# Six weight tiles of lead instead of five for the first token tile in the second block

## The chip, the cores and the metric

The kernel runs on one core of one Trainium2 chip. The metric is the device time of one execution in microseconds (us), from the first to the last instruction of the core with what lies around them. The engines are named as the profile names them: PE (TensorE, matmuls), PEld (its weight loads), DVE (VectorE), ACT (ScalarE), POOL (GpSimd) and SP (SyncE, which issues most of the transfers).

## What is computed

Two transformer blocks stand behind one another, each of two layers, over 256 tokens of width 1024. The change touches only the second. It is, with every matmul in full float32 precision:

```python
def second_block(x, norm_gains, w_ffn_gate, w_ffn_up, w_ffn_down, w_in, w_out, diff_lambda, diff_subln_gain):
    for layer in range(DEPTH):                       # DEPTH = 2
        g = norm_gains[layer]
        h = rmsnorm(x, g[0])
        x = x + 0.5 * rmsnorm(swiglu(h, w_ffn_gate[layer, 0], w_ffn_up[layer, 0], w_ffn_down[layer, 0]), g[1])
        h = rmsnorm(x, g[2])
        x = x + rmsnorm(token_mixer(h, w_in[layer], w_out[layer], ...), g[3])
        h = rmsnorm(x, g[4])
        x = x + 0.5 * rmsnorm(swiglu(h, w_ffn_gate[layer, 1], w_ffn_up[layer, 1], w_ffn_down[layer, 1]), g[5])
    return x
```

swiglu is (silu(h Wg) * (h Wu)) Wd with an inner width of 2816. token_mixer projects h to queries, keys and values, runs three kinds of attention over them (dilated, differential, stick-breaking: attn_a, attn_b and attn_c in the code), and multiplies what they give by w_out.

## The kernel before, in words

**Token tiles and weight tiles.** The 256 tokens are two token tiles of 128, t0 and t1. All weights of both blocks lie in one stream of weight tiles of 128 x 1024 numbers, in the order of use. Tiles 0 to 63 belong to the first block. In the second block tiles 64 to 129 are the first FFN of layer 0, 130 to 161 its mixer (24 tiles of w_in, then 8 of w_out), 162 to 227 its second FFN, and 228 to 391 the same for layer 1. Each weight tile is used by t0 and by t1. Float32 precision comes from splitting: a weight tile arrives by DMA as `raw`, ACT casts it to its high part `whi`, and DVE subtracts to get the low part `wlo` (Stream.convert, line 341). One use of a weight tile by one token tile is then six matmuls of 512 columns: twice high by high, low by high and high by low. Below this is called a pass. In the names `u0`, `m0` and `y0` a matmul writes for t0 (`u` gate and up, `m` mixer projection, `y` down or output projection), and `u1`, `m1` and `y1` for t1.

**Slots.** Eight converted weight tiles fit in memory in the second block (WBUFS = 4 and WMORE = 4). Tile n takes the slot of tile n - 8, so its cast waits until t1, which comes last, has used tile n - 8. Four raw tiles can be under way (RAWB = 4).

**Who sets the order.** Sched (line 167) is a planner that runs when the kernel is built. It holds one generator for each token tile and a list of side jobs (norms, swiglu, attention), and an estimated clock for each engine. Each round it lets one token tile issue its next pass. Among those that may, the one in the earlier stage (`phase`) goes first, and within a stage t0. A token tile may not start a pass when it would be `lead` or more weight tiles ahead of the last one:

```python
                if pos[t] < len(W.widths):
                    if pos[t] - lo >= self.lead or pos[t] >= W.nconv:
                        continue
```

`pos[t]` is the next weight tile of t, `lo` the smaller of the two, and `W.nconv` the number of tiles converted so far. LEAD is 5. What the planner writes is the program's order; the framework below it then makes one queue for each engine, in which an instruction that it takes to be ready can come ahead of one that it takes to wait. Each engine works through its queue in that order.

**The seams.** At the end of an FFN or of the mixer each token tile goes through `norms` (line 497) and `prenorm` (line 454): ACT sums the squares of the two halves of y (`junk`), DVE multiplies y by the gains (`u_post`), computes a reciprocal root in some nine dependent instructions of one column (`rw`, `rs_y`, `rs_h`, `rs_t`), and adds to the residual (`x`); PE transposes x (`tpx`), DVE scales (`h_f`), ACT casts (`h_hi`), DVE subtracts (`h_lo`), and only then can PE start the next stage for this token tile. Conversions during this time are held to three tiles ahead of t0 (QUIET = 3). In the mixer, attn_b (line 865) ends with the matmuls `avb`, a chain on DVE over `o_b`, the transpose `tpm` and the parts `m_hi` and `m_lo`, on which the weight tiles 160 and 161 (layer 0) or 324 and 325 (layer 1) wait. In the FFN, swiglu (line 558) makes `sg`, transposes it (`tpg`) and splits it into `g`.

Of the kernel before, what the change touches and what calls it, by code (L numbers as in the profile page):

```python
# [1852 lines left out]
LEAD, WBUFS, WMORE, RAWB, W2, QZ, S4 = (5,4,4,4,10,2,16)  # L1853
# [3 lines left out]
def build(tc, a, wst, widths, n1, tab, ident, cols, rows, lamp, out):  # L1857
    nc = tc.nc
    with ExitStack() as ctx:
        def pool(name, bufs, **k):  # L1860
            return ctx.enter_context(tc.tile_pool(name=name, bufs=bufs, **k))


        pool("pad", 1).tile([P, PADS[0] // 4], F32, name="pad")
        wp, hp, work, rawp, cp = pool("wp", WBUFS), pool("hp", 2), pool("work", 2), pool("rawp", RAWB), pool("const", 1)
        small, psA = pool("small", 2), pool("psA", 1, space=PSUM)

        class PS:
            def tile(self, shape, dt, tag, name):
                return psA.tile(shape, dt, tag=tag, name=name, bufs={"ps": 6, "tp": 2}[tag])  # L1870

        X = [cp.tile([P, D], F32, name=f"x{t}") for t in range(2)]
        ones = cp.tile([P, P], F32, name="ones")
        nc.gpsimd.memset(ones, 1.0)
        idn = cp.tile([P, P], F32, name="ident")
        nc.gpsimd.dma_start(idn, ident)
        cl = cp.tile([P, cols.shape[1]], F32, name="cols")
        nc.gpsimd.dma_start(cl, cols)
        lp = cp.tile([P, 128], F32, name="subln")
        st = Stream(tc, wst, widths, rawp, wp, WBUFS, RAWB)  # L1880
        S = Sched(tc, st, LEAD)
        ps = PS()
        one = ExitStack()
        p1 = one.enter_context(tc.tile_pool(name="first", bufs=1, reuse_waits="tile"))
        first = First(tc, S, X, cl, idn, ones, ps, work, small, hp, p1, a, [0, n1 // 2])
        second = Second(tc, S, X, cl, rows, idn, lp, ones, out, ps, work, small, hp)
        first.end = second.first
        left = [0, 1]

        def main(t):  # L1890
            yield from first.main(t)
            left.remove(t)
            if not left:
                assert all(x[1].__name__ == "prenorm" for x in S.sides), S.sides
                one.close()
                p2 = ctx.enter_context(tc.tile_pool(name="second", bufs=1, reuse_waits="tile"))
                second.open(p2, tab)
                second.lambdas(lamp[:, :256])
                st.widen(st.alloc(p2, WMORE), WMORE)
                st.rawb = RAWB  # L1900
            yield from second.main(t)

        first.consts()
        S.spawn(first.start())
        st.widen(lambda i: [first.s4([P, 1024], f"w{n}{i}", F32R) for n in range(2)], WX[0], WX[1], WX[2])
        mains = {t: main(t) if t < 2 else first.main(t) for t in range(4)}
        nc.gpsimd.dma_start(lp, lamp[:, 256:].to_broadcast([P, 128]))
        S.run(mains)
# [37 lines left out]
```

## Time and profile before

| | us |
|---|---|
| median of 3 runs | 1449.67 (1449.08 to 1450.29) |
| the profiled execution | 1447.77 |
| its span, first to last instruction | 1446.0 |
| PE busy | 1403.1 (97%) |
| DVE busy | 1002.7 (69%) |
| ACT busy | 765.8 (53%) |
| start of the second block in the span | about 426 |

The busy time of PE counts a matmul from its start to its modelled end. Matmuls overlap: one of 512 columns shows about 0.39 us but the next starts 0.23 us later, so time on PE is best read from the starts of neighbouring matmuls. Most of the arithmetic goes through two helper lines (L230 matmuls, L221 DVE, L216 ACT), so the rows below are told apart by the names of the tiles.

### The profile page before, as it was taken

The page shows a single profiled execution, that of the slowest core. Times are in us where ns is not written, and L with a number is a line of the kernel's source. Part 1 is how long each engine was busy: PE and PEld are TensorE (multiplying, and loading weights), DVE is VectorE, ACT ScalarE, POOL GpSimd, SP SyncE. Part 2 cuts the span into 40 slices and gives each one's busy share as a digit, 9 for nine tenths or more (in the row PEclk, how much of TensorE's full clock was granted, in tenths as well). Part 3 has the DMA queues.
Part 4 walks back from the last instruction along what each step waited for, and adds up shares of the span by engine and source line. Part 5 has one row for each costly group of instructions (what it writes and reads, how often), then busy time and mean ns, then how long its engine had stood idle before and what let it go on. Part 6 is the DMA issues. An engine that isn't in the chain of part 4 may idle for free.

```text
span 1446.0 us, 19092 instructions
## 1 busy us (share of the span) xinstructions
PE 1403.1 (97%) x6766; PEld 1134.5 (78%) x6766; DVE 1002.7 (69%) x2175; ACT 765.8 (53%) x1348; POOL 30.0 (2%) x46
## 2 busy tenths in 40 slices
PE   7999997999999999999999999999999999999997
PEld 4778886777877888777878888788887778788886
DVE  4899978779787555587886555765555878865554
ACT  4465533576565444567655444554445676554442
POOL 1000000000000000000000000000000000000000
PEclk9999999999999999999999999999999999999999
DMA  8751455333456555653446566566566534466551
GB/s 304 238 172 59 128 192 162 123 124 121 159 189 209 186 188 188 190 186 121 139 139 204 189 180 186 173 193 187 188 189 189 182 125 134 143 200 186 185 186 58
DMA packets 69088, 245.64 MB, mean 170 GB/s; under 512 B 7841, under 2 KB 8097, under 8 KB 68865
## 3 DMA queue, kind: packets, MB, share of 16 engines
q1 hardware_dynamic: 66384, 235.11, 51.1%
q0 software_dynamic: 2176, 8.79, 1.8%
q8 instruction: 53, 0.87, 0.2%
q10 hardware_dynamic: 432, 0.53, 0.1%
q14 instruction: 43, 0.34, 0.1%
HBM read 243.35 MB, written 1.05 MB: 169 GB/s over the span
## 4 chain that ended last, share of the span: by engine, by line
PE 79%; DVE 11%; DMA 4%; ACT 3%; issue 2%; SPq 0%; DVEq 0%; ACTq 0%
PE u L230 37%; PE y L230 18%; PE m L230 9%; DMA raw<-in_wst_dram 3%; PE yo L230 3%; DVE adaj L221 2%; DVE wlo L221 2%; PE av L230 2%; PE tpg L234 2%; DVE acc L221 1%; ACT whi L216 1%; PE tpp L234 1%; DMA ada<-in_adan_dram 1%; PE sc L230 1%; ACT f L216 1%
## 5 line engine op out<-in xcount | busy, mean ns | idle before, releaser
L221 DVE TENSOR_TENSOR wlo<-raw,whi 128x1024 fp32r<-128x1024 f32 (+1 forms) x380 | 459.2, 1211 | 341.8 <-ACT whi L216 339.4
L216 ACT CAST whi<-raw 128x1024 fp32r<-128x1024 f32 (+1 forms) x380 | 395.3, 1042 | 386.7 <-PE u L230 228.5
L230 PE MATMUL u<-whi,h_hi 128*128 128x512 f32 x704 | 281.2, 400 | 1.1 <-ACT h_hi L216 1.1
L230 PE MATMUL u<-whi,h_lo 128*128 128x512 f32 x704 | 275.0, 391 | 0.6 <-DVE h_lo L221 0.6
L230 PE MATMUL u<-wlo,h_hi 128*128 128x512 f32 x704 | 275.5, 392 | 0.0
L230 PE MATMUL y<-whi,g 128*128 128x512 f32 x704 | 218.3, 390 | 0.5 <-ACT g L216 0.5
L230 PEld LDWEIGHTS y<-whi,g 128*128 128x128 f32 x704 | 132.0, 188 | 28.8 <-ACT g L216 0.8
L230 PEld LDWEIGHTS u<-wlo,h_hi 128*128 128x128 f32 x704 | 132.1, 188 | 27.7
L230 PEld LDWEIGHTS u<-whi,h_lo 128*128 128x128 f32 x704 | 132.5, 188 | 27.1 <-DVE h_lo L221 2.5
L230 PEld LDWEIGHTS u<-whi,h_hi 128*128 128x128 f32 x704 | 132.2, 188 | 26.4 <-ACT h_hi L216 1.7
L230 PE MATMUL y<-wlo,g 128*128 128x512 f32 x352 | 137.3, 390 | 0.0
L230 PE MATMUL u<-whi,hhi 128*128 128x512 f32 (+2 forms) x256 | 98.7, 388 | 0.4 <-ACT whi L216 0.3
L221 DVE CUSTOM_DVE_ANT_0 adaj<-ada,cbc 128x1024 bf16<-128x1024 f32 x76 | 90.6, 1221 | 8.7 <-DMA ada<-in_ada_dram 8.6
L230 PE MATMUL u<-wlo,hhi 128*128 128x512 f32 (+2 forms) x256 | 94.4, 372 | 0.4 <-DVE wlo L221 0.4
L230 PE MATMUL u<-whi,hlo 128*128 128x512 f32 (+2 forms) x256 | 94.8, 372 | 0.0
L230 PE MATMUL m<-whi,h_hi 128*128 128x512 f32 x192 | 79.0, 415 | 0.4 <-ACT h_hi L216 0.4
L230 PEld LDWEIGHTS y<-wlo,g 128*128 128x128 f32 x352 | 66.1, 188 | 14.3
L230 PE MATMUL m<-wlo,h_hi 128*128 128x512 f32 x192 | 75.5, 395 | 0.0
L230 PE MATMUL m<-whi,h_lo 128*128 128x512 f32 x192 | 75.3, 394 | 0.0
L221 DVE SCALAR_TENSOR_TENSOR acc<-glu,cw,acc 128x512 f32<-128x512 f32 (+1 forms) x120 | 70.8, 613 | 0.0
L230 PEld LDWEIGHTS u<-whi,hhi 128*128 128x128 f32 x256 | 48.2, 189 | 8.3 <-issue 1.9
L230 PEld LDWEIGHTS u<-wlo,hhi 128*128 128x128 f32 x256 | 48.2, 188 | 8.0 <-DVE wlo L221 1.2
(294 smaller groups left out, 1961.6 us busy)
## 6 DMA issues: line engine op xcount, KB each, us to landing
raw<-in_wst_dram SPq DMA_DIRECT2D x376, 512.0 KB, 3.6
ada<-in_ada_dram SPq DMA_DIRECT2D x42, 512.0 KB, 4.3
grow<-in_rows_dram POOLq DMA_DIRECT2D x10, 512.0 KB, 5.1
raw<-in_wst_dram SPq DMA_DIRECT2D x8, 416.0 KB, 3.1
ada<-in_adan_dram SPq DMA_DIRECT2D x6, 512.0 KB, 5.3
raw<-in_wst_dram SPq DMA_DIRECT2D x8, 256.0 KB, 2.8
tab<-in_tab_dram POOLq DMA_DIRECT2D x1, 1536.0 KB, 8.4
x<-in_x_dram SPq DMA_DIRECT2D x2, 512.0 KB, 5.4
```

Of the source, the lines that this page charges most:

```text
L216: ins = getattr(self.nc.scalar, fn)(*a, **k)
L221: ins = getattr(self.nc.vector, fn)(*a, **k)
L230: self.nc.tensor.matmul(*a, **k)
L234: self.nc.tensor.transpose(out, in_, ident)
```

## The change

The planner's lead becomes 6 when the second block opens. Nothing else is edited.

```diff
                 st.widen(st.alloc(p2, WMORE), WMORE)
                 st.rawb = RAWB
+                S.lead = LEAD + 1
             yield from second.main(t)
```

The instructions of the second block are the same as before in number; their order is not. In the long middle of an FFN the two token tiles still alternate pass by pass, with t0 six tiles ahead instead of five. The order moves most at the seams.

**At the end of the first FFN of layer 0, on PE:** t0 ends with weight tile 129. Before:

```order
L230 MATMUL y0_0_4740<-whi129_5840,g_5853 128x512 x2
L230 MATMUL y0_0_4740<-wlo129_5841,g_5853 128x512
L230 MATMUL y0_1_4741<-whi129_5840,g_5853 128x512 x2
L230 MATMUL y0_1_4741<-wlo129_5841,g_5853 128x512
L230 MATMUL u1_5856<-whi125_5755,h_hi_4462 128x512
```

After:

```order
L230 MATMUL y0_0_4740<-whi129_5852,g_5841 128x512 x2
L230 MATMUL y0_0_4740<-wlo129_5853,g_5841 128x512
L230 MATMUL y0_1_4741<-whi129_5852,g_5841 128x512 x2
L230 MATMUL y0_1_4741<-wlo129_5853,g_5841 128x512
L230 MATMUL u1_5862<-whi124_5743,h_hi_4462 128x512
```

Behind t0's last pass t1 goes on with tile 124 instead of 125. Up to the transposes `tpx` of t0 four passes of t1 stand in the queue (124 to 127) instead of three. The last two of t1 (128 and 129) stand behind m0's tiles 130 to 133 instead of behind tile 130 and half of 131; and between t1's last pass and its own `tpx` there are now 5 matmuls, the four transposes `tpqk`, two passes and 2 matmuls (19 matmuls in all), where there were 25 matmuls.

**At the same seam, on DVE:** from the residual `x0` of t0 to the first conversion behind its norm. Before:

```order
L221 SCALAR_TENSOR_TENSOR x0_80<-u_post_5918,rs_y_5924,x0_80 128x512
L221 SCALAR_TENSOR_TENSOR x0_80<-u_post_5920,rs_y_5924,x0_80 128x512
L221 SCALAR_TENSOR_TENSOR h_f_5965<-tpx_5960,cols_86 128x512
L221 SCALAR_TENSOR_TENSOR h_f_5974<-tpx_5969,cols_86 128x512
L221 TENSOR_TENSOR h_lo_5938<-h_f_5965,h_hi_5937 128x512
L221 TENSOR_TENSOR h_lo_5938<-h_f_5974,h_hi_5937 128x512
L221 TENSOR_TENSOR wlo133_5992<-raw133_5863,whi133_5991 128x1024
```

After:

```order
L221 SCALAR_TENSOR_TENSOR x0_80<-u_post_5906,rs_y_5912,x0_80 128x512
L221 SCALAR_TENSOR_TENSOR x0_80<-u_post_5908,rs_y_5912,x0_80 128x512
L221 TENSOR_TENSOR wlo132_5936<-raw132_5850,whi132_5935 128x1024
L221 SCALAR_TENSOR_TENSOR sg_5945<-u1_5862,first_4637,sg_5945 128x256
L221 SCALAR_TENSOR_TENSOR h_f_5965<-tpx_5960,cols_86 128x512
L221 SCALAR_TENSOR_TENSOR h_f_5974<-tpx_5969,cols_86 128x512
L221 TENSOR_TENSOR h_lo_5926<-h_f_5965,h_hi_5925 128x512
L221 TENSOR_TENSOR h_lo_5926<-h_f_5974,h_hi_5925 128x512
L221 TENSOR_TENSOR wlo133_5986<-raw133_5869,whi133_5985 128x1024
```

The conversion of tile 132 and the `sg` of t1, which stood ahead of `x0`, now stand between `x0` and `h_f`. Further on, the two root chains (t0's second norm and t1's first), which stood interleaved with one another and with both `u_post` of t1, now follow one after the other, with the conversion of tile 136 and both `u_post` between them. The seam between the layers (tile 227) and the end of layer 1's first FFN (tile 293) are changed in the same way.

**At the end of the mixer of layer 0, on PE:** the transposes of t1's residual. Before, with t1's last matmul (`y1_1<-wlo161`) 38 matmuls ahead of the first row of `tpx`:

```order
L230 MATMUL u0_7370<-whi168_7296,h_hi_7222 128x512
L230 MATMUL u0_7370<-whi168_7296,h_lo_7223 128x512
L234 MATMUL tpx_7383<-ident_84,x1_81 128x128 x4
L230 MATMUL u0_7370<-wlo168_7297,h_hi_7222 128x512
L234 MATMUL tpx_7392<-ident_84,x1_81 128x128 x4
```

After:

```order
L230 MATMUL y1_1_7094<-wlo161_7034,m_hi_6998 128x512
L234 MATMUL tpg_7347<-ident_84,sg_7326 128x128
L230 MATMUL u0_7379<-whi168_7337,h_hi_7170 128x512
L230 MATMUL u0_7379<-whi168_7337,h_lo_7171 128x512
L230 MATMUL u0_7379<-wlo168_7338,h_hi_7170 128x512
L230 MATMUL u0_7379<-whi168_7337,h_hi_7170 128x512
L230 MATMUL u0_7379<-whi168_7337,h_lo_7171 128x512
L230 MATMUL u0_7379<-wlo168_7338,h_hi_7170 128x512
L230 MATMUL u0_7379<-whi169_7388,h_hi_7170 128x512
L230 MATMUL u0_7379<-whi169_7388,h_lo_7171 128x512
L234 MATMUL tpx_7398<-ident_84,x1_81 128x128 x4
L234 MATMUL tpx_7407<-ident_84,x1_81 128x128 x4
```

Behind t1's last pass there are now 8 matmuls of t0 ahead of t1's transposes instead of 38: t0's passes over tiles 162 to 167 stand ahead of t1's passes 160 and 161 now, where they stood behind them. Tiles 168 and 169 take the slots of 160 and 161.

**At the same seam, on DVE:** where the tail of t1's attn_b stands. Before:

```order
L221 TENSOR_TENSOR wlo163_7138<-raw163_6977,whi163_7137 128x1024
L221 TENSOR_TENSOR o_b_7156<-avb_7147,rdB_6869 128x2x64 x2
L221 TENSOR_TENSOR sq_b_7159<-o_b_7156 128x256
L221 TENSOR_REDUCE ssB_7161<-sq_b_7159 128x4
L221 TENSOR_SCALAR ssB_7161<-ssB_7161 128x4
```

After:

```order
L221 TENSOR_TENSOR h_lo_7171<-h_f_7219,h_hi_7170 128x512
L221 TENSOR_TENSOR wlo165_7231<-raw165_7101,whi165_7230 128x1024
L221 TENSOR_TENSOR wlo166_7237<-raw166_7134,whi166_7236 128x1024
L221 TENSOR_TENSOR wlo167_7243<-raw167_7181,whi167_7242 128x1024
L221 TENSOR_TENSOR o_b_7259<-avb_7250,rdB_6919 128x2x64 x2
L221 SCALAR_TENSOR_TENSOR rw_7296<-ss_7223 128x1
```

The tail of t1's attn_b, which stood ahead of t0's norm, now stands behind it and behind the conversions of tiles 165 to 167. The end of layer 1's mixer is changed in the same way.

## Rows read from the trace of the kernel before

**Rows 1.** The page: busy time of PE, share of the span.

```profile
PE 1403.1 (97%) x6766; PEld 1134.5 (78%) x6766; DVE 1002.7 (69%) x2175; ACT 765.8 (53%) x1348; POOL 30.0 (2%) x46
```

**Rows 2.** Windows: stretch, its length, busy us by engine (instructions), PE clock, DMA share.

```profile
core 0: us, PE busy (x) PEld busy (x) DVE busy (x) ACT busy (x) POOL busy (x), PEclk, DMA share, GB/s
425.00:608.00 183.00, 181.53 (x817) 147.15 (x816) 107.00 (x166) 88.78 (x119) 2.37 (x3) 1.00 0.62 199
608.00:631.00 23.00, 21.88 (x104) 17.28 (x103) 22.36 (x59) 13.74 (x29) 1.58 (x3) 1.00 0.65 222
...
616.00:631.00 15.00, 15.00 (x73) 12.52 (x73) 14.77 (x41) 7.14 (x17) 0.83 (x2) 1.00 0.70 245
...
631.00:734.70 103.70, 103.02 (x550) 83.41 (x550) 79.96 (x235) 68.12 (x131) 5.73 (x6) 1.00 0.42 132
734.70:755.70 21.00, 20.10 (x97) 16.28 (x96) 20.56 (x57) 12.05 (x25) 0.53 (x1) 1.00 0.49 160
755.70:924.00 168.30, 168.30 (x758) 137.06 (x757) 91.27 (x114) 81.73 (x109) 0.00 (x0) 1.00 0.60 188
```

**Rows 3.** Timeline, end of the first FFN, PE: start us, us, instruction [idle before].

```profile
607.97 0.39 PE L230 MATMUL u<-whi,h_hi 128*128 128x512 f32 x1
...
609.33 0.62 PE L230 MATMUL y<-whi,g 128*128 128x512 f32 x2
...
612.95 1.29 PE L234 MATMUL tpx<-ident,x 128*128 128x128 f32 x8 [0.74 <-DVE x L221]
...
615.01 0.73 PE L230 MATMUL m<-whi,h_hi 128*128 128x512 f32 x2 [0.21 <-ACT h_hi L216]
615.74 0.50 PE L230 MATMUL m<-whi,h_lo 128*128 128x512 f32 x1
```

**Rows 4.** The same stretch, DVE.

```profile
607.66 1.23 DVE L221 TENSOR_TENSOR wlo<-raw,whi 128x1024 fp32r<-128x1024 f32 x1 [1.49 <-ACT whi L216]
608.81 1.28 DVE L221 SCALAR_TENSOR_TENSOR u_post<-y,grow 128x512 f32<-128x512 f32 x2
...
610.77 0.48 DVE L221 SCALAR_TENSOR_TENSOR sg<-u,first,sg 128x256 f32<-128x256 f32 x1
...
612.05 1.41 DVE L221 SCALAR_TENSOR_TENSOR x<-u_post,rs_y,x 128x512 f32<-128x512 f32 x2
613.62 1.35 DVE L221 SCALAR_TENSOR_TENSOR h_f<-tpx,cols 128x512 f32<-128x512 f32 x2
```

**Rows 5.** The same stretch, ACT: squares of t0's first half, end of the second.

```profile
606.58 1.05 ACT L216 CAST whi<-raw 128x1024 fp32r<-128x1024 f32 x1 [1.67 <-PE u L230]
607.53 0.59 ACT L216 ACTIVATE junk<-y 128x512 bf16<-128x512 f32 x1
...
608.66 0.20 ACT L216 ACTIVATION_READ_ACCUMULATOR junk<-y 128x1 f32 x1
```

**Rows 6.** Timeline, end of the first mixer, PE.

```profile
734.71 0.39 PE L230 MATMUL y<-whi,m_hi 128*128 128x512 f32 x1
...
740.18 0.63 PE L234 MATMUL tpx<-ident,x 128*128 128x128 f32 x4 [0.90 <-DVE x L221]
...
755.71 0.40 PE L230 MATMUL u<-whi,h_hi 128*128 128x512 f32 x1
```

**Rows 7.** Timeline, the same seam, DVE: t1's attention tail, t0's norm, conversions.

```profile
732.17 0.49 DVE L221 TENSOR_TENSOR o_b<-avb,rdB 128x128 f32<-128x128 f32 x2 [1.43 <-PE avb L230]
...
738.32 0.42 DVE L221 TENSOR_TENSOR o_b<-o_b,subln 128x256 f32<-128x256 f32 x1
...
743.77 4.63 DVE L221 TENSOR_TENSOR wlo<-raw,whi 128x1024 fp32r<-128x1024 f32 x4
```

**Rows 8.** Timeline, the first block, PE: a long wait.

```profile
221.87 1.09 PE L234 MATMUL tpy<-ident,y 128*128 128x128 f32 x4 [3.54 <-DVE y L221]
```

**Rows 9.** Windows behind that wait of PE, and around a shorter one.

```profile
220.00:225.00 5.00, 3.13 (x10) 2.63 (x11) 5.00 (x10) 1.31 (x4) 0.00 (x0) 0.66 0.79 224
...
400.00:405.00 5.00, 3.17 (x21) 2.16 (x19) 3.14 (x9) 4.86 (x13) 0.00 (x0) 1.00 0.90 302
```

## The prediction

> **What bounds the kernel now.** I read the page first: PE is busy for 97% of the span [rows 1], so only its waits can be won or lost. The windows say where they are. In the long middle of an FFN PE never rests: 168.30 us of 168.30 [rows 2], and the stretches from 947 to 1114 us and from 1262 to 1434 us read the same. The change cannot win anything there. What is open lies at five seams: three ends of an FFN (608 to 631 us; those from 924 and from 1114 us read alike, PE lacking 1.1 us in each) and two ends of a mixer (734.7 to 755.7 us; 1241.2 to 1262.2 us is its twin, 0.9 us each) [rows 2]. The reader is to see the DVE column there: 22.36 of 23 us and 20.56 of 21 us. At a seam DVE is as full as PE, since two norms and the conversions meet on it; elsewhere it is at half load. PE gets through a seam nearly without loss because enough passes stand in its queue while DVE works. Last come the timelines of one seam of each kind [rows 3 to 7], which carry the sum.
>
> **Prices.** A pass is 609.33 - 607.97 = 1.36 us [rows 3]. A conversion takes 1.05 us on ACT, then 1.23 us on DVE [rows 4, 5], 2.3 us together. The norm of a token tile takes from the first u_post to x 3.24 us (612.05 - 608.81; about 2.95 without the sg inside) and to tpx 4.1 us [rows 3, 4]. From h_f to the first matmul that reads h_lo it is 615.74 - 613.62 = 2.1 us [rows 3, 4].
>
> **The middle of the FFN: 0.** With a lead of 6, a weight tile's slot is freed four passes (5.4 us) before t0 needs the new tile, where it was six (8.2 us). The 2.3 us conversion is the work under this cover. Were the cover gone, each of the 328 tiles would cost what is missing; 3 us of it remain, so I take nothing. swiglu stands as far behind its unit as before.
>
> **An FFN's end.** Time 0 is the end of t0's last pass (607.97 in the trace).
> - *t0's norm.* Before, PE comes to the matmul with h_lo at 7.77 us. Of this, three passes (4.1), ten transposes (1.1) and two matmuls (0.45) are work, so about 2.1 us are lost. After, the cover is four passes (5.4 us), one conversion less stands before u_post, which can start at about 1.0, and x is done at 5.4. So tpx no longer waits: 0.9 us gained. But a conversion (1.2 us) and sg (0.5 us) now stand on DVE between x and h_f, where nothing stood: h_f starts at 7.1 to 7.4, the matmul with h_lo at 9.3, with 7.0 us of work. Lost: 2.3 to 2.5. The gain is given back: +0.3.
> - *t1's norm.* Before it costs nothing: PE is busy for 15.00 of the 15 us from 616 us [rows 2], since 25 matmuls stood ahead of tpx. After, 19 matmuls and four transposes do: 4.8 us. What is needed is longer. u_post must wait for the conversion of tile 136, which waits for t1's pass over 128: it starts 1.1 us after t1's last pass. With 3.0 us to x, a copy of 0.6 us inside the chain, and 0.9 us to tpx, that is 5.6 to 5.9: 1.0 us lost. Then DVE has x's second half (0.5) and a conversion (1.2) before h_f, and 2.1 us more to h_lo: 3.9 us after tpx, under which there are 2.0 us of work (eight transposes, 5 matmuls). Another 1.9. Sum 3.0.
> So +3.3 for each of the two seams into a mixer. At the seam between the layers sg and g of the next FFN stand in DVE's queue as well: +3.8. **Together +10.4.** From below, t1's part can be nearly 0 (if DVE interleaves in time what the queue has in a row); from above it is all of t1's norm uncovered, about 4 us. I keep 5 to 15 for the three.
>
> **A mixer's end.** Time 0 is the end of t0's last pass (734.71). Before, t1 starts its FFN at 755.71 [rows 6]; of the 21.0 us thirteen passes (17.7) and 18 transposes (2.0) are work: 1.3 us lost, nearly all at tpx [rows 6]. After, by steps:
> 1. t0's norm: u_post starts at 1.5 (scores of attn_b and a conversion precede it), tpx at 5.6, four passes 5.4: 0.2.
> 2. tile 164's conversion stands before h_f: 3.9 us from tpx to the matmul with h_lo, 2.2 us of work: 1.7. The last two avb wait on ACT behind both squares: 0.3.
> 3. t1's attention tail on DVE now follows h_lo (4.5 us after tpx) and three conversions (3.5 us; 4.63 for four [rows 7]), so o_b starts at 8.0. It took 738.74 - 732.17 = 6.6 us before, with a conversion and both u_post inside (2.5): 4.1. tpm at 12.2; PE arrives at 12.1: 0.1. Then m_hi and m_lo: 1.0.
> 4. t0 meanwhile stops at tile 167, since 168 takes the slot of 160, which t1 has not used. After t1's pass over 160 the conversion takes 2.3 us against 1.9 us of work: 0.4.
> 5. t1's norm: on ACT the cast of 169 and g come before the squares (1.05, 0.4 and 1.3 us; squares and cast in [rows 5]), so u_post starts 1.9 and ends 3.1 us after t1's last pass, x comes 2.0 later, tpx at 6.0. Work until then: 2.4 us with the wait of step 4, where there were 38 matmuls (8.6 us). Lost: 3.6. Then, as at the FFN's end, a conversion before h_f: 1.9.
> Sum 9.2, less 1.3: +7.9, twice **+15.8**. From below: were tpm as early as before, steps 3 and 4 fall away and step 5 halves, +4 each. From above: 1.2 us more for the root chains that share DVE in step 3 and 1.3 for x's second half, +10.5 each. So 8 to 21.
>
> **Inside the mixers and at the start.** The order shifts there too, and no row of before shows a weight tile that came late. From below, PE's lack inside a mixer is 0.7 us [rows 2], so at most 1.4 for both can be won, and 1.5 between 425 and 608 us. From above, the two conversions that follow t1's start have 3.2 us of work as cover and a root chain of 2 us ahead of them on DVE: up to 2 us each. I take 0, nearest to the rows, and keep -3 to +4.
>
> **Sum.** 10.4 + 15.8 = 26.2 us. The profiled execution took 1447.77 us (span 1446.0 and 1.8 around it), so 1474; the median of the runs lies 1.9 us above it, so **1476**.
>
> **The rivals.**
> - *Faster, 1444 us.* The fourth pass of t1 covers t0's norm at all five seams, and nothing comes late in its place. Won: 1.2 us (0.9 and the break in tpx) at each of three seams, 1.1 at two, 5.8 in all. It decides at t1's tpx: if x of t1 is there within 4.8 us of its last pass at an FFN's end and 2.4 us at a mixer's end. For it speaks that waits for x are the largest of PE's waits; against it that no norm in these rows runs in under 4.1 us from u_post alone. 7%.
> - *Slower by less, 1466 us.* The mixers' ends cost what I say, the FFN ends even out because DVE finds gaps for the conversions. DVE at 97% before [rows 2] speaks against it. 22%.
> - *Slower by more, 1480 us.* The wait of 3.6 us in step 5 lowers PE's clock. In the first block PE waited 3.54 us, and the stretch of 5 us behind it has a mean clock of 0.66; the one from 245 us, behind a like wait, reads the same, while the stretch from 400 us, with 1.8 us idle in it, stays at 1.00 [rows 8, 9]. [...] 22%.
> [...]
> - *No change.* That the lead would not bind is excluded by the order, in which t0 stands six ahead; that all shifts cancel: 4%.
>
> **How the numbers follow.** The forecast itself 45%, the rivals as given. Faster by over 0.2% (about what a measurement of this kernel can tell from no change) 0.07, within 0.2% 0.04, slower 0.89. The range runs from the lower bounds with part of the gain inside (+8, 1458) to the upper bounds with the clock (+38, 1488); it leaves out the faster case and no change, 1 in 10, and some of the tails.
>
> **What would show it.** In the windows, the middles of the FFNs stay at full PE. Each of three FFN ends shows a wait of tpx for x near t1's norm, which was not there, and none at t0's first tpx but one for h_hi behind it. Each mixer's end shows waits for tpm's m_hi, for whi or wlo of 168, and one of over 3 us at t1's tpx. If t1's tpx waits under 1 us there, step 5 is wrong and the result lies near 1460; if conversions show up as PE's releasers in the middle of the FFNs, the cover of 3 us was an illusion and the result is above the range.

## The result and the profile after

The changed kernel takes 1467.54 us (median, 1464.85 to 1467.97) against 1449.38 in the same comparison: ratio 1.0122, interval 1.0105 to 1.014. It is 18 us slower.

The page's busy times, after; before is in [rows 1]:

```profile
span 1465.8 us, 19121 instructions
...
PE 1415.2 (97%) x6766; PEld 1138.2 (78%) x6766; DVE 1011.8 (69%) x2175; ACT 763.3 (52%) x1348; POOL 30.0 (2%) x46
```

Each engine runs as many instructions as before, and the shares hardly move. The page can't tell where 20 us of span went; the windows can. After, the stretches that answer to [rows 2], cut at the same places in the work (columns as there):

```profile
core 0: us, PE busy (x) PEld busy (x) DVE busy (x) ACT busy (x) POOL busy (x), PEclk, DMA share, GB/s
428.50:609.90 181.40, 179.48 (x803) 144.97 (x802) 104.77 (x163) 87.45 (x118) 2.38 (x3) 1.00 0.61 196
609.90:637.00 27.10, 24.74 (x113) 18.79 (x112) 25.11 (x59) 15.03 (x31) 1.59 (x3) 1.00 0.65 208
637.00:735.90 98.90, 98.82 (x525) 80.14 (x524) 77.58 (x222) 64.85 (x126) 5.73 (x6) 1.00 0.42 134
735.90:766.20 30.30, 26.49 (x124) 20.76 (x122) 25.56 (x72) 15.69 (x31) 0.53 (x1) 0.94 0.40 126
766.20:933.30 167.10, 167.10 (x750) 135.54 (x749) 89.77 (x111) 79.11 (x104) 0.00 (x0) 1.00 0.59 186
```

PE still never rests in the middle of an FFN (167.10 of 167.10 us from 766.2 us on). It lacks 2.36 us at the FFN's end, where it lacked 1.12, and 3.81 us at the mixer's end, where it lacked 0.90; the clock column there reads 0.94. Inside the mixer the lack fell from 0.68 to 0.08.

**A ledger by equal work.** A matmul is known, by its place in the kernel's order, by its weight tile and token tile, so its start can be compared between two traces, each counted from the first matmul of the second block. These first matmuls are, before and after:

```profile
426.05 0.48 PE L230 MATMUL u<-whi,h_hi 128*128 128x512 f32 x1
```

```profile
428.47 0.48 PE L230 MATMUL u<-whi,h_hi 128*128 128x512 f32 x1
```

The 2.4 us between them arose in the first block, which no edit here reorders; in the profiles of this study that start lies between 424.1 and 428.7 us. So a median says no more than some 2 us about the second block, and the ledger, from one profile of each kernel, says more. Where t1 is one weight tile further behind at the marker, a pass (1.36 us) is taken off; with lead 4, where it is one tile less behind, a pass is added. The table gives the us lost against before, from t1's matmuls with tiles 116, 140, 214, 280, 304 and 380; the sum goes on to the block's last matmul, so it holds what lies behind tile 380 as well:

| kernel | start | FFN end, layer 0 | mixer 0 | seam of layers | FFN end, layer 1 | mixer 1 | sum |
|---|---|---|---|---|---|---|---|
| forecast | 0 | 3.3 | 7.9 | 3.8 | 3.3 | 7.9 | 26.2 |
| changed kernel | 1.2 | 2.2 | 5.0 | 2.3 | 1.8 | 4.9 | 17.4 |

From the start of the second block to its last matmul it is 1029.4 us after and 1012.0 before: 17.4. So all five seams lose, as forecast, each less than forecast.

**The waits of PE in the second block, after:**

```profile
engine line waited for: us in total, times, longest us
PE tpx L234 <- DVE x L221: 7.6, 5, 3.2
PE tpg L234 <- DVE h_f L221: 2.8, 3, 0.9
...
PE u L230 <- DVE h_lo L221: 1.1, 4, 0.3
PE u L230 <- DVE wlo L221: 0.9, 3, 0.4
PE m L230 <- DVE wlo L221: 0.8, 2, 0.4
```

Two of the five waits for x are the long ones behind the mixers, three are t1's at the FFN ends. The transposes tpg that wait for h_f stand right behind t0's tpx.

**An FFN's end, DVE, after** (t0's last pass ends at 610.15, t1's at 627.0):

```profile
613.98 1.42 DVE L221 SCALAR_TENSOR_TENSOR x<-u_post,rs_y,x 128x512 f32<-128x512 f32 x2
615.32 1.22 DVE L221 TENSOR_TENSOR wlo<-raw,whi 128x1024 fp32r<-128x1024 f32 x1
616.45 0.48 DVE L221 SCALAR_TENSOR_TENSOR sg<-u,first,sg 128x256 f32<-128x256 f32 x1
616.85 1.28 DVE L221 SCALAR_TENSOR_TENSOR h_f<-tpx,cols 128x512 f32<-128x512 f32 x2
...
626.74 1.23 DVE L221 TENSOR_TENSOR wlo<-raw,whi 128x1024 fp32r<-128x1024 f32 x1 [0.91 <-ACT whi L216]
627.88 1.28 DVE L221 SCALAR_TENSOR_TENSOR u_post<-y,grow 128x512 f32<-128x512 f32 x2
...
631.45 1.41 DVE L221 SCALAR_TENSOR_TENSOR x<-u_post,rs_y,x 128x512 f32<-128x512 f32 x2
632.78 1.22 DVE L221 TENSOR_TENSOR wlo<-raw,whi 128x1024 fp32r<-128x1024 f32 x1
634.03 1.29 DVE L221 SCALAR_TENSOR_TENSOR h_f<-tpx,cols 128x512 f32<-128x512 f32 x2
```

and PE there:

```profile
615.60 1.03 PE L234 MATMUL tpx<-ident,x 128*128 128x128 f32 x8
617.58 0.44 PE L234 MATMUL tpg<-ident,sg 128*128 128x128 f32 x2 [0.95 <-DVE h_f L221]
...
618.96 0.50 PE L230 MATMUL m<-whi,h_lo 128*128 128x512 f32 x1
...
632.35 1.29 PE L234 MATMUL tpx<-ident,x 128*128 128x128 f32 x8 [0.36 <-DVE x L221]
634.05 0.50 PE L230 MATMUL m<-wlo,h_hi 128*128 128x512 f32 x1 [0.42 <-DVE wlo L221]
```

The reader is to see three conversions (`wlo`) in the norms' chains: between t0's x and h_f, ahead of t1's u_post, and behind t1's x.

**A mixer's end, PE, after:**

```profile
753.30 0.41 PE L234 MATMUL tpm<-ident,o_b 128*128 128x128 f32 x2 [0.19 <-DVE o_b L221]
...
754.17 0.74 PE L230 MATMUL y<-whi,m_hi 128*128 128x512 f32 x2 [0.23 <-ACT m_hi L216]
...
758.01 0.50 PE L230 MATMUL u<-wlo,h_hi 128*128 128x512 f32 x1 [0.23 <-DVE wlo L221]
...
762.83 1.94 PE L234 MATMUL tpx<-ident,x 128*128 128x128 f32 x8 [3.16 <-DVE x L221]
```

t1's passes 160 and 161 stand here behind tpm; [rows 6] had t0's tpx at this place with 0.90. Then t1's tpx waits 3.16 us, and the window behind it runs at half clock (0.50); from 765.9 to 771 us the granted clock is 1.00 again:

```profile
762.50:765.90 3.40, 3.08 (x11) 2.73 (x12) 3.25 (x6) 1.46 (x4) 0.00 (x0) 0.50 0.46 123
```

### The profile page after: what moved, and what is told of

It reads as the page before. It is cut to its first block, busy times and chain, and to the rows that moved or that the text cites. A ratio compares the mean times of both kernels' runs of the same rounds, so it can differ in the third digit from the quotient of the medians.

```text
span 1465.8 us, 19121 instructions
## 1 busy us (share of the span) xinstructions
PE 1415.2 (97%) x6766; PEld 1138.2 (78%) x6766; DVE 1011.8 (69%) x2175; ACT 763.3 (52%) x1348; POOL 30.0 (2%) x46
## 4 chain that ended last, share of the span: by engine, by line
PE 72%; DVE 15%; ACT 5%; DMA 5%; issue 2%; SPq 0%; DVEq 0%; ACTq 0%
PE u L230 33%; PE y L230 17%; PE m L230 8%; DVE wlo L221 3%; DMA raw<-in_wst_dram 3%; PE yo L230 3%; DVE adaj L221 2%; ACT whi L216 2%; PE tpg L234 2%; PE av L230 1%; DVE acc L221 1%; DVE rs_t L221 1%; DVE x L221 1%; DVE rs_y L221 1%; DMA ada<-in_adan_dram 1%
## 5 line engine op out<-in xcount | busy, mean ns | idle before, releaser
L230 PE MATMUL u<-whi,h_hi 128*128 128x512 f32 x704 | 275.8, 392 | 0.3 <-ACT h_hi L216 0.2
L230 PE MATMUL y<-whi,g 128*128 128x512 f32 x704 | 224.1, 399 | 0.5 <-ACT g L216 0.5
L230 PEld LDWEIGHTS y<-whi,g 128*128 128x128 f32 x704 | 126.9, 188 | 23.9 <-ACT g L216 0.7
```

Of the source, the lines that this page charges most:

```text
L230: self.nc.tensor.matmul(*a, **k)
```

## The experiments

Lead by place is written as a function `at` of the weight tile that a token tile is about to use:

```diff
-                    if pos[t] - lo >= self.lead or pos[t] >= W.nconv:
+                    if pos[t] - lo >= self.at(pos[t]) or pos[t] >= W.nconv:
```

The ledger of all eleven runs, in us against before as above (for three of them only the sum is given); the last column is the difference of the medians to the runs of before beside them:

| kernel | start | FFN end 0 | mixer 0 | layers | FFN end 1 | mixer 1 | sum | medians |
|---|---|---|---|---|---|---|---|---|
| lead 6, not in the mixers | 1.4 | 1.9 | 0.4 | 2.2 | 1.6 | 0.3 | 7.8 | 6.8 |
| lead 6, only in the mixers | 0.2 | 0.2 | 4.6 | 0.1 | -0.2 | 4.9 | 9.8 | 11.5 |
| lead 6, FFN middles | | | | | | | 1.1 | 2.0 |
| busy in the wait | 1.2 | 2.2 | 5.0 | 2.3 | 1.8 | 4.9 | 17.4 | 18.1 |
| lead 7, FFN middles | | | | | | | 1.5 | 1.5 |
| QUIET 2, lead 6 | 1.6 | 0.3 | 9.2 | 0.1 | -0.3 | 8.9 | 19.8 | 18.5 |
| lead 4 | 0.3 | 5.1 | 10.9 | 6.1 | 4.9 | 11.3 | 37.9 | 37.5 |
| lead 6, mixer hearts | 0.4 | 0.2 | 3.8 | 0.1 | -0.1 | 5.5 | 9.8 | 10.7 |
| norm after the tail | 1.9 | 2.2 | 11.5 | 2.4 | 1.9 | 11.3 | 31.1 | 27.9 |
| not in mixers, QUIET 2 at FFN ends | 0.9 | 0.4 | 0.4 | 0.1 | 0.1 | 0.3 | 2.3 | 4.2 |
| lead 5, QUIET 2 at FFN ends | | | | | | | 1.2 | 1.4 |

**Halves of the change: FFN ends and mixers.**

```diff
-                S.lead = LEAD + 1
+                S.at = lambda p: LEAD if 136 <= p < 172 or 300 <= p < 336 else LEAD + 1
```

> Lead 6 in the second block, but 5 from weight tile 136 to 171 and from 300 to 335. The order of the three FFN ends is then that of the changed kernel, the order of the two mixer ends that of the kernel before. If the cost of the change is a sum over the seams, this keeps the FFN ends' part. The forecast's sum gives +10.4 us over the kernel before (1460). The trace of the changed kernel, read by equal work, shows 6.2 us for the three FFN ends and 1.0 at the start: +7 (1456.5). The rival in which the FFN ends even out gives 0 to +1 (1450). At t1's tpx behind the mixer's end there is no wait of 3 us, and no stretch at the lower clock.

```diff
-                S.lead = LEAD + 1
+                S.at = lambda p: LEAD + 1 if 136 <= p < 172 or 300 <= p < 336 else LEAD
```

> The other half: lead 6 from weight tile 136 to 171 and from 300 to 335 only, 5 elsewhere. The FFN ends have the order of the kernel before, the mixer ends that of the changed kernel. The forecast's sum gives +15.8 us without the clock (1465). The trace of the changed kernel gives +13.1 at the two ends, with two stretches of 3.4 us at half clock in it (1.7 us each), less 2 to 4 us that the mixers' interiors seem to win: +9 to +11 (1459). If the halves add up, this and the run with lead 6 outside the mixers have together what the change costs, 18 us. If the wait of 3.3 us at t1's tpx came from the lead at the FFN's end before it and not from the mixer, it is absent here and the time is below 1453.

Measured: 1455.34 (ratio 1.0045, 1.003 to 1.006) and 1460.00 (1.008, 1.0063 to 1.0097), against 1448.54. The halves are 6.8 and 11.5 us and add up to the change's 18. In the ledger each half loses at its own seams and, but for 0.4 us, not at the other's. The FFN ends don't even out, so the rival of 1466 us had the time but not the reason; and the mixers' part needs the lead inside the mixers.

**The middle: lead 6 and lead 7.**

```diff
-                S.lead = LEAD + 1
+                S.at = lambda p: LEAD + 1 if 80 <= p < 120 or 180 <= p < 218 or 245 <= p < 284 or 340 <= p < 380 else LEAD
```

> Lead 6 only in the middles of the four FFNs (weight tiles 80 to 119, 180 to 217, 245 to 283, 340 to 379), 5 elsewhere; at every seam the order is that of the kernel before. The forecast takes the middle at nothing, since 5.4 us of cover stand over a conversion of 2.3 us: 1449.4 within 1.5 us. If a slot that is freed one pass later costs something in each tile, the some 155 tiles pay: 0.1 us each would be +15.

For the other, LEAD + 2 stands in the place of LEAD + 1.

> Lead 7 in the middles of the four FFNs only (weight tiles 80 to 119, 180 to 217, 245 to 283, 340 to 379), 5 elsewhere. It tests the price of the cover. A slot is freed two passes (2.7 us) before t0 needs the new tile, against a conversion of 2.3 us. If the forecast's account of the cover is right, 0.4 us of it are left, PE stays full in the middles, and the time is that of the run with lead 6 there, 1450.5 within 1.5. If what lies between the engines takes more than 0.4 us in each tile, all some 155 tiles pay the difference: 0.2 us each would be +30 us, and PE waits for whi and wlo in the middles.

Measured: 1450.54 against 1448.54 (1.0011, 1.0002 to 1.0021), and 1449.43 against 1447.95 (1.0012, 0.9997 to 1.0027). By the ledger 1.1 and 1.5 us for four goings in and out. With lead 7, one middle reads

```profile
480.00:583.00 103.00, 103.00 (x464) 83.78 (x463) 54.30 (x61) 47.75 (x63) 0.00 (x0) 1.00 0.61 188
```

PE is full. A slot freed two passes ahead (2.7 us) is enough for a conversion of 2.3 us, as the forecast's price of the cover has it.

**The clock by itself.** Twelve matmuls that nothing uses are put into t1's wait:

```diff
             tp = self.psum("tp", "tpx")
+            if t == 1 and j == 2 and n == 0:
+                wh = self.W.get(self.pos[0] - 1)[0]
+                for i in range(12):
+                    self.nc.tensor.matmul(tp, self.h[0][0][:, i % KT, :], wh[:, :512], start=True, stop=True)
```

> The changed kernel, with 12 matmuls of 512 columns that nothing uses put into PE's queue between t1's last pass and its tpx at each of the two mixer ends: 2.8 us of work inside the wait of 3.3 us. Everything else stands as in the changed kernel. If the half-clock stretch of 3.4 us comes because PE rested for 3.3 us, it does not come here, and the time is 1.7 us shorter at each seam: 1464.1 where the changed kernel takes 1467.5. If the stretch has another cause, 1467.5. If x of t1 is late by less than the 2.8 us in this run, the matmuls cost something themselves: up to 1470.

Measured: 1466.60 (1.0119, 1.0104 to 1.0134), no gain that shows. Yet the slow stretch is gone. PE at the first mixer's end, and the two windows before and behind the wait that is left:

```profile
752.75 3.01 PE L466 MATMUL tpx<-whi,h_hi 128*128 128x512 f32 x12
...
758.42 1.38 PE L234 MATMUL tpx<-ident,x 128*128 128x128 f32 x8 [0.85 <-DVE x L221]
760.22 0.50 PE L230 MATMUL u<-wlo,h_hi 128*128 128x512 f32 x1 [0.41 <-DVE wlo L221]
```

```profile
752.00:757.90 5.90, 5.57 (x25) 4.20 (x24) 4.64 (x14) 2.87 (x7) 0.53 (x1) 1.00 0.36 101
757.90:761.50 3.60, 2.48 (x12) 1.51 (x12) 3.46 (x5) 1.37 (x4) 0.00 (x0) 1.00 0.45 146
```

So the rest of PE did bring the slow stretch, as the forecast's third rival had it: 0.50 behind a wait of 3.16 us, 1.00 behind one of 0.85. But t1's first `u` comes 761.53 - 424.13 = 337.4 us after the start of the block here, 766.18 - 428.47 = 337.7 in the changed kernel: the slow stretch cost 0.3 us there, not 1.7, and at the second mixer's end 0.2. By the next markers nothing is left of this gain, as the two ledger rows are the same. Behind tpx PE has only eight transposes and four matmuls until h_hi is there. At full clock the transposes take 1.38 us and it waits 0.41 us in between; at half clock, in the changed kernel, they take 1.94 and the trace shows no wait there.

**What the FFN ends cost: conversions in the norms' chains.**

```diff
-QUIET = 3
+QUIET = 2
```

> The changed kernel with conversions held to two tiles ahead of t0 during a norm, where it was three. At an FFN's end this takes the conversion of the tile three ahead out of the stretch between t0's x and h_f, and lets the first u_post of t1 go ahead of the conversion that stood before it; one conversion still stands between t1's x and h_f. If those conversions in the norms' chains are what the FFN ends cost, the 2.1 us of each fall to some 0.7, and the time is 1467.5 - 4 = 1463.5. If it is the smaller number of passes ahead of t1's tpx, or the lead as such, the time stays at 1467.5. The mixer ends keep their order, with the wait of over 3 us at t1's tpx.

Measured: 1466.49 (1.0133, 1.0114 to 1.0152), no gain. The ledger says why: the three FFN ends fell from 2.2, 2.3 and 1.8 us to 0.3, 0.1 and -0.3, nearly all of their cost, and the mixers rose from 5 to 9. There the tail of t1's attention comes later still, and PE waits for it (2.18 us at the first tpm) as well as at t1's tpx (2.93); behind each of the two waits the matmuls of 512 columns start 0.43 us apart (753.17 to 756.16 us, 764.02 to 765.73), as in the changed kernel's window at 0.50 (765.12 to 765.55), and not 0.23. The sum is that of the second expectation, for a reason that neither had; for the seam the first was right. Next, QUIET 2 where it helps, with lead 5 in the mixers:

```diff
+        S.q = QUIET if j == 3 else QUIET - 1
...
-            if self.S.quiet and self.nconv >= max(self.S.pos.values()) + QUIET:
+            if self.S.quiet and self.nconv >= max(self.S.pos.values()) + self.S.q:
```

> Lead 6 but 5 in and around the mixers (the first experiment, 1455.3 against 1448.5), with conversions held to two tiles ahead of t0 during the norms of the FFNs, three during those of the mixers. The mixer ends have the order of the kernel before. If the three FFN ends cost what they do (6.4 us) because of the conversions that stand in the norms' chains, all or nearly all of it goes: 1449 to 1451, with 1.2 us left that lead 6 costs at the start of the block. If it is the lead itself, 1455.

Measured: 1452.74 (1.003, 1.002 to 1.004). The FFN ends fall from 5.7 us to 0.6 together; the ledger's sum from 7.8 to 2.3, the median only from 1455.34 to 1452.74, within what the first block adds. In DVE's timeline the conversion has left the stretch between t0's x and h_f, and DVE now waits for PE:

```profile
613.44 0.75 DVE L221 SCALAR_TENSOR_TENSOR x<-u_post,rs_y,x 128x512 f32<-128x512 f32 x1
614.10 0.48 DVE L221 SCALAR_TENSOR_TENSOR sg<-u,first,sg 128x256 f32<-128x256 f32 x1
615.03 1.29 DVE L221 SCALAR_TENSOR_TENSOR h_f<-tpx,cols 128x512 f32<-128x512 f32 x2 [0.45 <-PE tpx L234]
```

**The same with lead 5**, as a version that might beat both (`S.at` gives LEAD throughout).

> The kernel before (lead 5) with the same two tiles at the FFN ends: a version that might beat both. One conversion leaves the stretch between t1's x and h_f at three seams, where the kernel before has no wait that the trace shows, so little can be won: 0 to 1.5 us, 1447 to 1448.5 where the kernel before takes 1448.5. If a conversion is late behind it, up to 1 us lost each, 1451.

Measured: 1449.95 against 1448.53 (1.0008, 1.0000 to 1.0017). Nothing is won, the ledger has 1.2 us lost.

**The other way.** `S.at` gives LEAD - 1 throughout.

> The other way: lead 4 in the second block. Slots come free a pair of passes earlier than with 5, so no conversion can be late. If the cost of lead 6 were one of slots and of cover, lead 4 would cost nothing: 1449 or a little less. If it is one of the order at the seams (the norm of one token tile needs passes of the other beside it, and t1's attention tail must come before t0's norm), it costs too: at the mixers' ends the tail stands behind t0's norm here as well, with four passes of t0 ahead of t1's passes 160 and 161 and none ahead of its tpx: some 4 to 6 us at each, 1458 to 1462.

Measured: 1485.41 (1.026, 1.0239 to 1.028), 37 us slower, three times what was expected, although slots come free earlier. Each FFN end loses 5 to 6 us and each mixer 11. t1's tpx has hardly anything of t0 ahead of it, and waits. This is the first FFN end, and below it the first mixer's end:

```profile
626.99 1.29 PE L234 MATMUL tpx<-ident,x 128*128 128x128 f32 x8 [2.26 <-DVE x L221]
```

```profile
763.84 1.94 PE L234 MATMUL tpx<-ident,x 128*128 128x128 f32 x8 [5.21 <-DVE x L221]
```

A stretch at half clock stands behind such a wait here too (0.50 from 762.0 to 768.8 us at this mixer's end); how much of the 37 us it makes was not taken apart. With slots that come free earlier and a larger loss here, and with the full middles above, the cost of lead 6 isn't one of slots, but for the 0.4 us that PE loses ahead of wlo of 168 at a mixer's end. Five lies between two losses.

**The mixer's end: work ahead of tpx, or the late tail?**

```diff
-                S.lead = LEAD + 1
+                S.at = lambda p: LEAD + 1 if 136 <= p < 146 or 300 <= p < 310 else LEAD
```

> Lead 6 from weight tile 136 to 145 and from 300 to 309 only, 5 elsewhere, so t0 is five ahead again at the mixer's end. The tail of t1's attention still stands behind t0's norm there, but 17 matmuls of t0 stand between t1's last pass and its tpx instead of 8. If the 3.3 us at this tpx come from too little work between them, 9 matmuls more (2.1 us) leave a wait of 1.2 to 1.7 us at each mixer's end, no stretch at half clock, and some 2.5 us of the 5 that a mixer costs: 1454. If the late tail alone sets the time of t1's first u, whatever stands ahead of tpx, each mixer costs the same 5 us: 1459.

Measured: 1458.64 (1.0076, 1.0057 to 1.0094). The wait at t1's tpx is 1.37 us, as expected with 17 matmuls ahead of it instead of 8, but a mixer still costs 3.8 and 5.5 us. What tpx no longer waits stands at t0's norm, since the `avb` that filled it stands earlier:

```profile
742.44 0.73 PE L230 MATMUL u<-whi,h_hi 128*128 128x512 f32 x2 [1.21 <-ACT h_hi L216]
743.72 0.50 PE L230 MATMUL u<-whi,h_lo 128*128 128x512 f32 x1 [0.55 <-DVE h_lo L221]
...
757.91 1.29 PE L234 MATMUL tpx<-ident,x 128*128 128x128 f32 x8 [1.37 <-DVE x L221]
```

Then the tail's place on DVE was put right in the changed kernel:

```diff
-        S.spawn(self.norms(t, ys, l, 3, 1.0, ev))
+        S.spawn(self.after_tail(t, ys, l, ev))
...
+    def after_tail(self, t, ys, l, ev):
+        if t == 0:
+            yield self.tails[1, l]
+        yield from self.norms(t, ys, l, 3, 1.0, ev)
```

`self.tails[1, l]` is the event that ends t1's attn_b.

> The changed kernel, with t0's norm at the two mixer ends planned only after the tail of t1's attn_b. On DVE the tail's o_b stands ahead of t0's u_post, as it did in the kernel before, and on PE t1's passes 160 and 161 stand ahead of t0's tpx. If the place of the tail behind t0's norm in DVE's queue is what a mixer's end costs, the 6 us there fall to 1 or 2, and the time is some 1458 to 1460. If the tail is late by itself (its avb stands between t1's passes 158 and 159, where it stood ahead of 156), PE waits for tpm and m_hi ahead of pass 160 instead, t0's norm follows later still, and the time stays at 1467 or rises by some us.

Measured: 1476.47 (1.0189, 1.0173 to 1.0204), 9 us more than the changed kernel. The wait went to the tail:

```profile
737.33 1.95 PE L230 MATMUL avb<-v,pTB 128*128 128x128 f32 x16
...
746.25 0.66 PE L234 MATMUL tpm<-ident,o_b 128*128 128x128 f32 x2 [5.58 <-DVE rs_y L221]
747.37 1.22 PE L230 MATMUL y<-whi,m_hi 128*128 128x512 f32 x2 [0.46 <-ACT m_hi L216]
...
752.65 1.27 PE L234 MATMUL tpx<-ident,x 128*128 128x128 f32 x8
```

Not all of the 9 us is the order. Behind this wait the matmuls of 512 columns start 0.43 us apart (748.39 to 752.23 us), as in the changed kernel's window at 0.50, and t1's two passes 160 and 161 take 752.65 - 747.37 = 5.3 us, where two passes take 2.7 at full clock: some 2.6 us at this end go with the slow clock. But with the tail put ahead of the norm PE waits 5.58 us for the tail all the same. So the order of tail and norm is not the whole cause; the tail itself is late. Its beginning shows by how much. The last scores of t1's attn_b on PE, before and after (the last matmuls `scb` ahead of the mixer's end):

```profile
722.63 1.13 PE L230 MATMUL scb<-kT,qz 128*128 128x256 f32 x4
...
738.88 0.41 PE L234 MATMUL tpm<-ident,o_b 128*128 128x128 f32 x2
```

```profile
732.73 1.03 PE L230 MATMUL scb<-kT,qz 128*128 128x256 f32 x4
```

and in the last experiment:

```profile
729.83 1.03 PE L230 MATMUL scb<-kT,qz 128*128 128x256 f32 x4
```

Before, they stand 734.71 - 722.63 = 12.1 us ahead of the end of t0's last pass, after 735.9 - 732.7 = 3.2 us, with lead 6 only in the mixer's heart 5.0 us. From these scores to tpm it takes 738.88 - 722.63 = 16.3 us before and 746.25 - 729.83 = 16.4 in the last experiment; in the changed kernel it takes 753.30 - 732.73 = 20.6, so the place behind t0's norm adds some 4 us to the tail there. With 3.2 us of lead, m_hi and m_lo cannot be there until 13 us after t0's end, and all work that t1 has by then is four passes, 5.4 us; in the changed kernel t0's passes 162 to 167 fill the rest, and are then missing ahead of t1's tpx. The scores fall back by 10.1 us, where t1's projections fall back by 4.2 (its first matmul with tile 153 moved from 716.94 to 721.13); counted from the block's first matmul it is 7.7 and 1.8. The delay is there in full at the first of the four heads of t1's attn_b, whose scores start at 702.8 us before and at 713.1 after. From there to the last head it takes 19.8 us before and 19.7 after. So attn_b begins late as a whole. It waits for attn_a (line 871 of the kernel before); what holds it up there was not taken apart, and this cause stays open.

## Why the prediction was right, and where its sizes were off

The direction, the five places, the waits named and the range held; the forecast of 1476 is 8 us above. In the profile the sum is 17.4 us where 26.2 stood: the FFN ends cost 6.3 of 10.4 and the mixers 9.9 of 15.8, and 1.2 stand at the start, where nothing was forecast. Both large terms were set too high. Point by point:

- **Middle of the FFN, 0.** Right, also with lead 7.
- **FFN end, t0's norm, +0.3.** tpx no longer waits, and the conversion and sg do stand ahead of h_f, which starts 6.7 us after t0's end, where 7.1 to 7.4 was forecast. PE comes to the matmul with h_lo at 618.96 - 610.15 = 8.8 us, where 9.3 was forecast; with the forecast's 7.0 us of work that is 1.8 lost, against 2.1 before. So -0.3.
- **FFN end, t1's norm, +3.0.** u_post waits for the conversion that waits for the cast, as written; tpx comes 5.3 us after t1's last pass (forecast 5.6 to 5.9), the matmul with h_lo 3.8 us later (3.9). The chain was right. 0.5 us are lost at tpx, not 1.0, and 1.7 behind it, not 1.9: 2.2. With t0's norm 1.9 of 3.3. QUIET 2 shows that conversions in the chains make up nearly all of it. The 0.5 more at the seam of the layers wasn't there (2.3 against 2.2).
- **Mixer's end.** By steps, forecast and measured loss, the latter from the starts of neighbouring matmuls (0.23 us for one of 512 columns, 0.11 for a small one): t0's tpx 0.2 and 0; t0's h_lo 2.0 and 0.4; tpm with m_hi 1.1 and 0.9; wlo of 168 0.4 and 0.4; t1's tpx 3.6 and 3.3, what is behind it 1.9 and 1.6. Together 6.6 of 9.2. In the forecast's own way of counting, the end lasts 30.3 us, of which fourteen passes (19.0) and 38 small matmuls and transposes (4.2) are work: about 7 us lost, against 1.3 before. **The step that failed is the second**: fourteen small matmuls and transposes of t1's attention (`avb`, `tpp`) stand between t0's tpx and the first matmul with h_lo. In the kernel's order they are eight, but in the trace each of these `avb` stands twice. With eight transposes and two matmuls that is 2.9 us of work, where I had counted 2.2, and the matmul with h_lo came after 3.3 us, where I had 3.9. The reason that I gave for step 5, 8 matmuls instead of 38 ahead of tpx, gives the size of that one wait. It is not the cause of the loss: with 17 matmuls the wait shrinks and the loss stays. That the tail would be late was in step 3, as a matter of its place on DVE; that its scores already begin 9 us closer to t0's end was in no step.
- **Interior of the mixers and start, 0 within -3 to +4.** About -0.7 in each mixer (the first end loses 5.7 more than before, the ledger has 5.0 for interior and end, and PE's lack inside the mixer fell by 0.6) and +1.2 at the start, inside the bounds.
- **The clock.** The stretch came where the rival had it, at 0.50 for 3.4 us instead of 0.66 over 5. The rival's 1480 takes 3.4 us for two such stretches, my estimate from the 0.66 in [rows 9] (a third of 5 us at each seam). No run shows this term: what they showed is 0.3 us at t1's first u at the first mixer's end, 0.2 at the second, and nothing by the next marker, since PE had nothing to be late with. Where two passes stood behind the wait of 5.58 us, as in the last experiment, the slow stretch took 2.6 us of PE's time at one seam.

## What to carry to other kernels

A lead between two streams of work isn't only a question of buffers: between 4 and 6, with hardly a slot late, it cost this kernel 18 us one way and 37 the other through the order at the seams. When one stream runs further ahead, ask first for the longest side chain of the one behind (here attention, scores to projection 16 us) and whether it still begins early enough, then which background jobs (here conversions) slide into the chains of the norms. A wait that is filled or moved without shortening the chain behind it comes back elsewhere (here 3.16 us as 1.21, 0.55 and 1.37, or as 5.58).

## What the runs showed of the hardware

A stretch at half clock also followed shorter waits than the 3.16 us of the changed kernel. With lead 6 only in the mixers' hearts, where the expectation had no such stretch, the waits at the mixer's end are 1.21, 0.55 and 1.37 us, and the window behind the last reads

```profile
759.40:763.00 3.60, 3.38 (x9) 2.70 (x10) 3.42 (x10) 2.44 (x6) 0.00 (x0) 0.53 0.51 152
```

and with lead 4 it is 0.50 from 748.3 to 751.7 us, behind waits of 1.25 and 0.39 us; behind the wait of 2.26 us the matmuls of 512 columns there start 0.43 us apart (630.07 to 632.21 us), later 0.23. The kernel before, with waits of 0.9 us at its seams, shows 1.00 in every window of [rows 2]. No run was made to find how short a wait such a stretch still follows.
